# Layer 0's input projection as a one-level Strassen product, with the sums of the weights kept in DRAM

## The chip, the cores and the metric

The kernel runs on one core of one Trainium2 chip. The metric is the device time of one execution in microseconds (us); a kernel's time is the median of its runs. Names of engines follow the profile: PE is TensorE (PEld its weight loads), DVE is VectorE, ACT is ScalarE, POOL is GpSimd, SP is the queue from which all transfers are issued.

## The reference, cut to what matters

One step of a decoder trunk with two layers, all in float32, over 4096 prompt rows and 8 rows of samples, 1024 wide. The change is in layer 0:

```python
def even_layer(x, pool_prefix, conv_prefix, pos0, g_norm, w_in, pool_w, pool_scale, conv_w, w_out):
    h = rms_norm(x, g_norm)
    p = jnp.einsum('btd,de->bte', h, w_in)               # 1024 -> 3072
    u, z_a, b_gate, c_gate, v_in, z_b = jnp.split(p, EVEN_SPLITS, axis=-1)   # 512 each
    d = pool_mix(u, pool_prefix, pos0).reshape(B, T, N_POOL_GROUPS, POOL_GROUP)
    y_a = jnp.einsum('btgc,gce->btge', d, pool_w).reshape(B, T, W_POOL) * pool_scale * jax.nn.silu(z_a)
    v = c_gate * v_in
    y_b = b_gate * short_conv(v, conv_prefix, conv_w) * jax.nn.silu(z_b)
    y = jnp.einsum('bte,ed->btd', jnp.concatenate([y_a, y_b], axis=-1), w_out)
    ...
    return x + y, new_pool, new_conv
```

`pool_mix` is a trailing mean over 2, 4, 8 or 16 rows, by group of 128 channels; `short_conv` has three taps along the rows. Layer 1 is sliding-window attention with its own projections; its code is the same before and after.

## The kernel before

Every float32 operand of a product is split into two parts (`split`: ACT rounds it to the high part, DVE subtracts that to get the low part, L69 and L72), and a product is three matmuls: high by high, high by low, low by high.

Layer 0 goes through the 4096 rows in six chunks (`L1_CHUNKS`), of 512, 768, 768, 768, 640 and 640 rows; the 8 samples ride with the first. For each chunk, three stages follow one another:

- `prep`: 128 rows at a time are loaded, normed (ACT squares and sums, POOL makes the reciprocal root in `rstd`, DVE scales by it and by the gain row `gb`), transposed by PE eight blocks at a time, and split into `hh` and `hl`, channels on the partitions, rows along the free side.
- `mixers`: in each of four groups, six blocks of 128 output columns are projected (`block`: lines 259 to 261). A block loads a granule of weights (1024 by 128, 512 KB, buffers `wr`, three of them), splits it (`wh`, `wl`, four each), and multiplies it with the chunk in two pieces of at most 512 columns, 24 matmuls each. A piece is gathered in a PSUM bank `ps`, and ACT or DVE takes it from there into the pooling, the convolution and the gates. `psd` is the small block-diagonal product of the pooling branch. The result is split into `yh` and `yl`.
- `outproj`: the chunk's output projection (lines 385 to 389), 512 columns wide, with eight granules of `w_out` per chunk. While it runs, `prep` of the next chunk runs as well: its transposes stand between the output products on PE.

A scheduler sets the order of each engine's instructions when the kernel is built; each engine then works strictly in its order and waits at an instruction whose inputs are not there. Buffers are rings: a new tile waits until the old one in its place is done with.

Of the kernel before, what the change touches and what calls it, by code (L numbers as in the profile page):

```python
# [54 lines left out]
def hybrid_kernel(  # L55
# [85 lines left out]
    # ------------------------------------------------------------------ layer 0  # L141
    with ExitStack() as l1:
# [10 lines left out]
        gb = c1.tile([P, D], F32, tag="gb", name="gb")  # L153

        def load_w(src, shape, raw=None):
            if raw is None:
                raw = wp.tile([P, *shape], F32, tag="wr", name="wr", bufs=3)
                sp.dma_start(raw, src)
            wh = wp.tile([P, *shape], F32R, tag="wh", name="wh", bufs=4)
            wl = wp.tile([P, *shape], F32R, tag="wl", name="wl", bufs=4)  # L160
            split(wh, wl, raw)
            return wh, wl
# [44 lines left out]
        first_w = []  # L207

        def prep(ci):
            t0, n = L1_CHUNKS[ci]  # L210
            cols = n + (NS if ci == 0 else 0)
            hh = hp.tile([P, KT, cols], F32R, tag="hh", name="hh")
            hl = hp.tile([P, KT, cols], F32R, tag="hl", name="hl")
            for i in range(n // P):
                if not early:
                    xt = xp.tile([P, D], F32, tag="x", name="xt", bufs=2)
                    sp.dma_start(xt, xp_flat[t0 + i * P:t0 + (i + 1) * P, :])
                else:
                    xt = early.pop(0)
                if ci == 0 and i == 0:  # L220
                    first_w.append(load_w(w_in[:, :, 0:P], [KT, P], first_raw))
                ht = xp.tile([P, D], F32, tag="hn", name="ht", bufs=1)
                normed(xt, ht, P, gb, sm, hl[:, :, i * P:(i + 1) * P])
                to_channels(ht, pt, hh, hl, i * P)
# [1005 lines left out]
```

## Time and profile before

| what | value |
| --- | --- |
| three runs | 3395.51, 3397.54, 3399.41 us |
| median | 3397.54 us |
| span of the profiled execution, first to last instruction | 3388.8 us |
| the median less that span (start and end around it) | 8.7 us |
| PE busy | 95% of the span |
| DVE, ACT, POOL busy | 64%, 50%, 22% |
| end of layer 0's last output product on PE | 1541.0 us |

The profiled execution's own time is not listed apart from the three runs; it is taken as its span and the 8.7 us around it, which makes the median. Busy time is the time in which at least one instruction runs on the engine. Matmuls overlap one another, so a busy PE does not say how fast it goes; the time of a matmul is read as the length of a stretch divided by the matmuls in it.

### The profile page before, as it was taken

How to read it: one execution, taken by the hardware profiler on the slowest of the kernel's cores; microseconds unless marked ns; L12 is line 12 of the kernel's file. 1: busy time of each engine (PE TensorE's matmuls, PEld its weight loads, DVE VectorE, ACT ScalarE, POOL GpSimd, SP SyncE). 2: the span in 40 equal slices, each digit the busy share in tenths (PEclk: the TensorE clock that was granted, in tenths of full speed). 3: DMA queues.
4: the chain of work that ended last, by engine and by line, in shares of the span. 5: the costliest groups of instructions: out<-in, count | busy, mean ns of one | idle time of the engine just before them, and what ended most of it. 6: DMA issues, size and time to landing. Idle time of an engine off the chain costs nothing.

```text
span 3388.8 us, 48608 instructions
## 1 busy us (share of the span) xinstructions
PE 3224.2 (95%) x17226; PEld 2797.9 (83%) x17226; DVE 2152.4 (64%) x4348; ACT 1682.7 (50%) x3930; POOL 742.5 (22%) x1183
## 2 busy tenths in 40 slices
PE   7999999999999999998989999999999999999877
PEld 7989989988998999996767778777777887776665
DVE  4544443443443453443698897988979889797863
ACT  3332222231222232223586785867858678575761
POOL 1000000000000000001233342533425334343420
PEclk9999999999999999999999999999999999999988
DMA  5352243234224224234312424224232242321212
GB/s 159 100 160 65 63 131 100 63 100 125 62 76 155 75 88 137 73 101 131 104 53 75 136 68 135 87 82 135 68 126 90 81 139 71 108 83 58 74 66 97
DMA packets 303421, 330.19 MB, mean 97 GB/s; under 512 B 21545, under 2 KB 208561, under 8 KB 303138
## 3 DMA queue, kind: packets, MB, share of 16 engines
q1 hardware_dynamic: 303177, 327.09, 30.8%
q8 instruction: 136, 2.23, 0.3%
q14 instruction: 108, 0.88, 0.1%
HBM read 293.04 MB, written 36.29 MB: 97 GB/s over the span
## 4 chain that ended last, share of the span: by engine, by line
PE 44%; DVE 16%; ACT 7%; DMA 5%; issue 3%; POOL 1%; SPq 1%; DVEq 0%; ACTq 0%; POOLq 0%
PE pst L539 6%; PE pst L540 6%; PE pst L541 6%; PE ps L259 5%; PE ps L261 5%; PE ps L260 5%; ACT s L808 3%; DVE wl L507 3%; PE pso L389 2%; PE pso L385 2%; PE pso L387 2%; DVE qt L72 1%; PE o L842 1%; DVE s L792 1%; DVE st L802 1%
## 5 line engine op out<-in xcount | busy, mean ns | idle before, releaser
L259 PE MATMUL ps<-hh,wh 128*128 128x384 f32 (+3 forms) x2304 | 732.8, 318 | 4.0 <-ACT wh L69 3.7
L261 PE MATMUL ps<-hh,wl 128*128 128x384 f32 (+3 forms) x2304 | 731.7, 318 | 1.0 <-DVE wl L72 1.0
L260 PE MATMUL ps<-hl,wh 128*128 128x384 f32 (+3 forms) x2304 | 732.2, 318 | 0.1
L69 ACT ACTIVATE wh<-wr 128x1024 fp32r<-128x1024 f32 (+1 forms) x320 | 281.3, 887 | 727.5 <-PE ps L260 330.1
L72 DVE TENSOR_TENSOR wl<-wr,wh 128x1024 fp32r<-128x1024 f32 (+1 forms) x320 | 321.2, 1012 | 369.8 <-ACT wh L69 347.7
L259 PEld LDWEIGHTS ps<-hh,wh 128*128 128x128 f32 x2304 | 434.3, 189 | 5.2 <-ACT wh L69 4.3
L261 PEld LDWEIGHTS ps<-hh,wl 128*128 128x128 f32 x2304 | 433.8, 188 | 1.5 <-DVE wl L72 1.5
L260 PEld LDWEIGHTS ps<-hl,wh 128*128 128x128 f32 x2304 | 434.2, 188 | 0.6 <-DVE hl L72 0.4
L507 DVE SCALAR_TENSOR_TENSOR wl<-wr,gt,wh 128x256 fp32r<-128x256 f32 (+1 forms) x448 | 278.1, 638 | 67.8 <-ACT wh L506 61.6
L539 PE MATMUL pst<-wh,hh 128*128 128x512 f32 x768 | 312.0, 406 | 0.5 <-DVE xr L75 0.4
L506 ACT ACTIVATE wh<-wr,gt 128x256 fp32r<-128x256 f32 (+1 forms) x448 | 250.8, 597 | 116.0 <-DMA wr<-in_w_in_odd_dram 66.7
L541 PE MATMUL pst<-wl,hh 128*128 128x512 f32 x768 | 304.4, 396 | 0.0
L540 PE MATMUL pst<-wh,hl 128*128 128x512 f32 x768 | 303.9, 396 | 0.0
L808 ACT ACTIVATE s<-s,st,rq 128x128 f32<-128x128 f32 x512 | 246.9, 483 | 34.0 <-DVE st L804 32.3
L828 POOL TENSOR_SCALAR_AFFINE_SELECT qh<-ph 128x512 fp32r<-128x512 f32 x124 | 90.3, 728 | 688.4 <-ACT ph L69 669.9
L627 PE MATMUL psz<-hh,wh 128*128 128x512 f32 x512 | 211.6, 413 | 6.7 <-ACT wh L506 6.7
L539 PE MATMUL pst<-wh,yh 128*128 128x512 f32 x512 | 211.6, 413 | 3.9 <-DVE xr L75 3.8
L385 PE MATMUL pso<-wh,yh 128*128 128x512 f32 x512 | 202.7, 396 | 5.3 <-DVE xr L75 4.9
L628 PE MATMUL psz<-hl,wh 128*128 128x512 f32 x512 | 207.1, 405 | 0.0
L629 PE MATMUL psz<-hh,wl 128*128 128x512 f32 x512 | 206.5, 403 | 0.0
L541 PE MATMUL pst<-wl,yh 128*128 128x512 f32 x512 | 204.8, 400 | 0.0
L540 PE MATMUL pst<-wh,yl 128*128 128x512 f32 x512 | 204.7, 400 | 0.0
(265 smaller groups left out, 6577.7 us busy)
## 6 DMA issues: line engine op xcount, KB each, us to landing
wr<-in_w_in_odd_dram SPq DMA_DIRECT2D x320, 256.0 KB
wr<-in_w_in_even_dram SPq DMA_DIRECT2D x144, 512.0 KB
wr<-in_w_out_odd_dram SPq DMA_DIRECT2D x128, 256.0 KB
wr<-in_w_out_even_dram SPq DMA_DIRECT2D x48, 512.0 KB
xr<-in_x_prompt_dram SPq DMA_DIRECT2D x64, 256.0 KB
x<-xr SPq DMA_DIRECT2D x64, 256.0 KB
xt<-x SPq DMA_DIRECT2D x32, 512.0 KB
xr<-x SPq DMA_DIRECT2D x64, 256.0 KB
```

The lines of the kernel that those rows point to most:

```text
L69: return act.activation(out, in_, AF.Copy)
L72: return dve.tensor_tensor(out=out, in0=a, in1=b, op=ALU.subtract)
L259: pe.matmul(ps, lhsT=wh[:, kt, :], rhs=xh, start=kt == 0, stop=False)
L260: pe.matmul(ps, lhsT=wh[:, kt, :], rhs=xl, start=False, stop=False)
L261: pe.matmul(ps, lhsT=wl[:, kt, :], rhs=xh, start=False, stop=kt == KT - 1)
L385: pe.matmul(acc[i], lhsT=yh[:, kt, ts_], rhs=wh[:, e, :], start=kt == 0, stop=False)
L506: act.activation(wh[ix], raw[ix], AF.Copy, scale=gt[:, kt:kt + 1])
L507: dve.scalar_tensor_tensor(out=wl[ix], in0=raw[ix], scalar=gt[:, kt:kt + 1], in1=f(wh[ix]), op0=ALU.mult, op1=ALU.subtract)
L539: pe.matmul(acc[i], lhsT=xh(kt), rhs=wh, start=kt == 0, stop=False)
L540: pe.matmul(acc[i], lhsT=xl(kt), rhs=wh, start=False, stop=False)
L541: pe.matmul(acc[i], lhsT=xh(kt), rhs=wl, start=False, stop=kt == KT - 1)
L808: C["exp"] = act.activation(s[:, h, :], s[:, h, :], AF.Exp, bias=nm[:, h:h + 1], scale=r4[:, h:h + 1], accum_out=den[:, h:h + 1])
```

## The change

The input projection of layer 0 is done as one level of Strassen's scheme (in Winograd's form). Two blocks of 128 output columns, the two halves of the 1024 channels, and the two halves of a chunk's rows make a 2 by 2 by 2 product of quarters; 8 quarter products become 7, with sums of quarters as operands. A chunk has 12 such pairs of blocks (`pair`), and each quarter product is 4 channel tiles by 3 matmuls, over half of the chunk's rows at once.

- The rows' side: `prep` makes seven operands of a pair of row tiles (`B11`, `B21`, `B22` and the sums `T1` to `T4`), in `operand_cols`, and splits each.
- The weights' side: `operands` makes four granules of a pair, `A11` and `A12`, `S2` and `S1`, `S3` and `S4`, `A22` (the last has half the size). In the first chunk it loads the two blocks, multiplies them by the norm's gain on POOL (`scaled`; the gain row `gb` on the rows' side is gone), makes the sums on DVE and POOL, splits them, and writes all seven quarters to DRAM (`wsc`). Later chunks load the seven quarters from there.
- The outputs: within a pair, bank `px` goes on being added to after it has been copied (by ACT: `p1`, `u2`; bank `pz` gives `p5`), and three of the four results are sums that DVE makes (`out11`, `out22`, `out12`); the fourth is `px` at the end.
- Chunks are 768, 768, 768, 768, 512 and 512 rows (`L0_CHUNKS`), so products are 384 columns wide in the first four (388 with the samples) and 256 in the last two. `wh` and `wl` have three buffers each, not four.

```diff
-L1_CHUNKS = [(0, 512), (512, 768), (1280, 768), (2048, 768), (2816, 640), (3456, 640)]
+L0_CHUNKS = [(0, 768), (768, 768), (1536, 768), (2304, 768), (3072, 512), (3584, 512)]
...
+        def scaled(raw):
+            v = raw.rearrange("p a k e -> p (a k) e")
+            pool.tensor_tensor(out=v, in0=v, in1=g0.unsqueeze(2).to_broadcast([P, KT, P]),
+                               op=ALU.mult)
...
+        def operands(ci, pair, blocks):
+
+            if ci > 0:
+                out = []
+                for i in range(4):
+                    raw = raw_tile()
+                    n = 1 if i == 3 else 2
+                    sp.dma_start(raw[:, :n], wsc[pair][:, 2 * i:2 * i + n])
+                    out.append(parts(raw[:, :n]))
+                return out
+            ra = first_w.pop(0) if first_w else load_block(blocks[0])
+            scaled(ra)
+            ga = parts(ra)
+            rb = first_w.pop(0) if first_w else load_block(blocks[1])
+            scaled(rb)
+            s12 = xp.tile([P, 2, 4, P], F32, tag="x", name="s12", bufs=2)
+            s34 = xp.tile([P, 2, 4, P], F32, tag="x", name="s34", bufs=2)
+            add(s12[:, 1], rb[:, 0], rb[:, 1])
+            sub(s12[:, 0], s12[:, 1], ra[:, 0])
+            pool.tensor_tensor(out=s34[:, 0], in0=ra[:, 0], in1=rb[:, 0], op=ALU.subtract)
+            sub(s34[:, 1], ra[:, 1], s12[:, 0])
+            sp.dma_start(wsc[pair][:, 0:2], ra)
...
+                b12 = temp("b12", 1)
+                acopy(b12, quad(0, 1))
+                q = quad(0, 0)
+                split(bh[:, 0, :, cs], bl[:, 0, :, cs], q)
+                t1 = temp("t4", 2)
+                sub(t1, b12, q)
+                q = quad(1, 1)
+                split(bh[:, 2, :, cs], bl[:, 2, :, cs], q)
+                t2 = temp("t4", 2)
+                sub(t2, q, t1)
+                part(0, t1)
+                t3 = temp("t4", 2)
+                sub(t3, q, b12)
+                part(1, t2)
+                part(2, t3)
+                q = quad(1, 0)
+                split(bh[:, 1, :, cs], bl[:, 1, :, cs], q)
+                t4 = temp("t4", 2)
+                sub(t4, q, t2)
+                part(3, t4)
...
-                        pe.matmul(ps, lhsT=wh[:, kt, :], rhs=xh, start=kt == 0, stop=False)
-                        pe.matmul(ps, lhsT=wh[:, kt, :], rhs=xl, start=False, stop=False)
-                        pe.matmul(ps, lhsT=wl[:, kt, :], rhs=xh, start=False, stop=kt == KT - 1)
...
+                    for kt in range(4):
+                        for i, (u_, v_) in enumerate(((wh, xh), (wh, xl), (wl, xh))):
+                            pe.matmul(ps, lhsT=u_[:, at, kt, :], rhs=v_[:, o, kt, :],
+                                      start=start and kt == 0 and i == 0, stop=kt == 3 and i == 2,
+                                      skip_group_check=True)
...
+                x = bank("px")
+                mm(x, "A11", "B11", start=True)
+                p1 = kept(x, "p1")
+                y = bank("py")
+                mm(y, "A12", "B21", start=True)
+                out11(y, p1)
+                if mid is not None:
+                    mid()
+                mm(x, "S2", "T2")
+                u2 = kept(x, "u2")
+                z = bank("pz")
+                mm(z, "S1", "T1", start=True)
+                p5 = kept(z, "p5")
+                mm(x, "S3", "T3")
+                out22(x, p5)
+                mm(z, "S4", "B22")
+                out12(z, u2)
+                mm(x, "A22", "T4")
+                return x
```

Three places in the order of the engines, first POOL at the program's start. `rnt` and `rnr` are the two steps of a row tile's reciprocal root, `u` and `vv` carry rows over from the last piece, and before the change the order there is this:

```order
L105 TENSOR_SCALAR rnt<-ss 128x1
L274 COPY u<-ucar 128x15
L326 COPY vv<-vcar 128x2
L109 TENSOR_TENSOR rnr<-rnt,mh 128x1
L105 TENSOR_SCALAR rnt<-ss 128x1
L109 TENSOR_TENSOR rnr<-rnt,mh 128x1
```

After the change, with L197 the multiplication of a weight block by the gain:

```order
L105 TENSOR_SCALAR rnt<-ss 128x1
L197 TENSOR_TENSOR wr<-wr,g_139 128x1024
L109 TENSOR_TENSOR rnr<-rnt,mh 128x1
L105 TENSOR_SCALAR rnt<-ss 128x1
L427 COPY u<-ucar 128x15
L109 TENSOR_TENSOR rnr<-rnt,mh 128x1
L197 TENSOR_TENSOR wr<-wr,g_139 128x1024
```

The multiplication of the first weight block has come between the two steps of the first row tile's reciprocal root; 24 of them stand in the first chunk's part of POOL's order, two to a pair of blocks.

The second place is PE at the program's start, before the change (`tr` and `trs` are the transposes of row tiles and of the samples):

```order
L260 MATMUL ps<-hl,wh 128x256
L261 MATMUL ps<-hh,wl 128x256
L130 MATMUL tr<-ident,ht 128x128 x8
L138 MATMUL trs<-ident,hts 128x8 x8
L259 MATMUL ps<-hh,wh 128x264
L260 MATMUL ps<-hl,wh 128x264
```

After the change, the first rows of all:

```order
L334 MATMUL tr<-ident,xe 128x128 x16
L334 MATMUL tr<-ident,xt 128x128 x32
L138 MATMUL trs<-ident,xs_344 128x8 x8
L373 MATMUL px<-bh,wh 128x388
L373 MATMUL px<-bl,wh 128x388
L373 MATMUL px<-bh,wl 128x388
```

Before, the first piece's products (256 wide) stand between the transposes, after 16 of them; now all 48 transposes and those of the samples stand ahead of the first product, since a product takes half of the chunk at once.

The third place is DVE in a late chunk, in the convolution's blocks of a group, before the change (640 rows, pieces 320 wide; the words in brackets name the engines that the instruction waits for):

```order
L72 TENSOR_TENSOR wl<-wr,wh 128x1024 [waits DMAHW4_49,Activation_49]
L333 SCALAR_TENSOR_TENSOR t<-vv,cw,t 128x320 [waits DVE_49] x2
L78 TENSOR_TENSOR t<-t,zb 128x320 [waits Activation_49]
L72 TENSOR_TENSOR wl<-wr,wh 128x1024 [waits DMAHW7_49,PE_49,Activation_49]
L78 TENSOR_TENSOR t<-t,zb 128x320 [waits DVE_49,Activation_49]
L78 TENSOR_TENSOR y<-ps,t 128x320 [waits DVE_49,PE_49]
```

After the change (512 rows, 256 wide; `yb<-px,p` is `out22` of a pair, `zb<-pz,u` its `out12`):

```order
L72 TENSOR_TENSOR wl<-wr,wh 128x512 [waits DMAHW4_49,PE_49,Activation_49]
L75 TENSOR_TENSOR zb<-py,p_10371 128x256
L78 TENSOR_TENSOR t<-t,zb 128x256 [waits Activation_49]
L72 TENSOR_TENSOR wl<-wr,wh 128x1024 [waits DMAHW5_49,PE_49,Activation_49]
L75 TENSOR_TENSOR yb_10431<-px,p_10417 128x256 [waits PE_49,Activation_49]
L75 TENSOR_TENSOR zb<-pz,u_10402 128x256 [waits PE_49]
L72 TENSOR_TENSOR wl<-wr,wh 128x1024 [waits DMAHW6_49,Activation_49]
```

New are the sums from the banks, and a weight split stands right ahead of `out22`, for which PE's last product of the pair (into `px` again) has to wait; before, a bank was written once and the next piece had another.

## Rows read from the trace of the kernel before

**Rows 1.** The page: the span and each engine's busy time over it.

```profile
span 3388.8 us, 48608 instructions
...
PE 3224.2 (95%) x17226; PEld 2797.9 (83%) x17226; DVE 2152.4 (64%) x4348; ACT 1682.7 (50%) x3930; POOL 742.5 (22%) x1183
```

**Rows 2.** Stretches of layer 0: us, each engine's busy time (instructions), granted clock, DMA.

```profile
core 0: us, PE busy (x) PEld busy (x) DVE busy (x) ACT busy (x) POOL busy (x), PEclk, DMA share, GB/s
120.00:170.00 50.00, 50.00 (x420) 50.00 (x419) 29.09 (x64) 14.96 (x29) 3.04 (x12) 1.00 0.29 86
237.91:442.00 204.09, 204.09 (x1178) 204.09 (x1177) 88.76 (x134) 51.10 (x81) 12.39 (x32) 1.00 0.24 72
442.00:518.04 76.04, 72.87 (x336) 58.11 (x336) 30.70 (x36) 21.96 (x34) 5.19 (x12) 1.00 0.46 146
1313.10:1485.71 172.61, 172.61 (x1179) 172.54 (x1178) 81.77 (x133) 47.10 (x80) 10.27 (x30) 1.00 0.29 87
1486.33:1541.03 54.70, 54.70 (x245) 45.25 (x243) 13.85 (x20) 10.17 (x20) 2.83 (x9) 1.00 0.34 115
```

**Rows 3.** The timeline's start: start us, us, engine, line, operation, tiles, [idle before <-releaser].

```profile
...
0.80 0.38 SPq L416 DMA_DIRECT2D xe<-in_x_prompt_dram  x1
...
4.38 1.06 ACT L120 ACTIVATE hl<-xe 128x1024 fp32r<-128x1024 f32 x1 [2.30 <-DMA xe<-in_x_prompt_dram]
...
6.76 1.28 DVE L122 SCALAR_TENSOR_TENSOR ht<-xe,rnr,gb 128x1024 f32<-128x1024 f32 x1 [6.76 <-POOL rnr L109]
...
8.10 1.97 PE L130 MATMUL tr<-ident,ht 128*128 128x128 f32 x8 [8.10 <-DVE ht L122]
...
9.77 1.06 ACT L69 ACTIVATE wh<-wr 128x1024 fp32r<-128x1024 f32 x1 [0.73 <-DMA wr<-in_w_in_even_dram]
...
15.79 0.58 PE L259 MATMUL ps<-hh,wh 128*128 128x256 f32 x1
```

**Rows 4.** VectorE groups by shape, layer 0: count | busy us, mean ns | idle before, releasers.

```profile
L72 DVE TENSOR_TENSOR wl<-wr,wh 128x1024 fp32r<-128x1024 f32 x192 | 234.2, 1222 | 307.3 <-ACT wh L69 301.4 <-DMA x<-xr 3.4 <-ACT hh L69 2.2
...
L72 DVE TENSOR_TENSOR hl<-tr,hh 128x512 fp32r<-128x512 f32 x64 | 41.3, 682 | 2.9 <-ACT hh L69 2.8
...
L78 DVE TENSOR_TENSOR vv<-ps,c 128x384 f32<-128x384 f32 x24 | 13.4, 558 | 38.5 <-PE ps L261 38.5
...
L78 DVE TENSOR_TENSOR vv<-ps,c 128x256 f32<-128x256 f32 x8 | 3.4, 425 | 5.9 <-PE ps L261 5.9
...
L579 DVE TENSOR_SCALAR xt<-xt,rnr 128x1024 f32<-128x1024 f32 x3 | 2.3, 754 | 3.0 <-POOL rnr L109 3.0
```

**Rows 5.** ScalarE groups by shape, layer 0, same columns.

```profile
L69 ACT ACTIVATE wh<-wr 128x1024 fp32r<-128x1024 f32 x192 | 202.8, 1059 | 627.5 <-PE ps L260 330.1 <-PE pso L387 195.8 <-issue 63.9
...
L69 ACT ACTIVATE c<-ps 128x384 f32<-128x384 f32 x24 | 11.6, 482 | 34.2 <-PE ps L261 34.2
...
L69 ACT ACTIVATE c<-ps 128x256 f32<-128x256 f32 x4 | 1.5, 381 | 5.5 <-PE ps L261 5.5
```

**Rows 6.** GpSimd instructions of three kinds: duration ns min/median/max.

```profile
L656 POOL TENSOR_TENSOR tab<-raw,gq x132: 309/326/1104, 1556.7 to 3191.7; 128x64 f32<-128x64 f32 x128, 8x64 f32<-8x64 f32 x4
...
L326 POOL COPY vv<-vcar x48: 186/187/194, 6.0 to 1468.9; 128x2 f32<-128x2 f32 x48
...
L828 POOL TENSOR_SCALAR_AFFINE_SELECT qh<-ph x124: 630/637/1627, 1709.5 to 3334.6; 128x512 fp32r<-128x512 f32 x124
```

**Rows 7.** A piece of the timeline in layer 1, VectorE and GpSimd.

```profile
2005.06 1.20 DVE L507 SCALAR_TENSOR_TENSOR wl<-wr,gt,wh 128x512 fp32r<-128x512 f32 x1
2005.08 0.63 POOL L828 TENSOR_SCALAR_AFFINE_SELECT ql<-pl 128x512 fp32r<-128x512 f32 x1
...
2005.78 0.97 POOL L830 TENSOR_SCALAR_AFFINE_SELECT pl<-pl 128x512 fp32r<-128x512 f32 x1
```

**Rows 8.** Two VectorE lines of layer 1: duration ns min/median/max.

```profile
L507 DVE SCALAR_TENSOR_TENSOR wl<-wr,gt,wh x448: 446/544/1196, 1544.8 to 3229.8; 128x256 fp32r<-128x256 f32 x86, 128x512 fp32r<-128x512 f32 x64
...
L792 DVE COPY_PREDICATED s<-pmask,sc x248: 407/440/461, 1695.4 to 3302.4; 128x256 f32<-128x256 uint8 x124
```

More of the change, by code (lines that the diff above doesn't have):

```diff
@@ L151, in hybrid_kernel @@
         pt = l1.enter_context(tc.tile_pool(name="pt1", bufs=2, space=PSUM))
[L153 to L162, printed above, removed]
         w_in = w_in_even[0].rearrange("(k p) e -> p k e", p=P)
         w_out = w_out_even[0].rearrange("(k p) e -> p k e", p=P)
+        wsc = [dram.tile([P, 7, 4, P], F32, tag=f"wsc{i}", name=f"wsc{i}") for i in range(12)]
+        AT = {"A11": (0, 0), "A12": (0, 1), "S2": (1, 0), "S1": (1, 1), "S3": (2, 0), "S4": (2, 1),
+              "A22": (3, 0)}
+        g0 = c1.tile([P, KT], F32, tag="g0", name="g0")
         pwl = c1.tile([P, 4, P], F32R, tag="pwl", name="pwl")
@@ L205, in setup_sample, with x_norm0 @@
             sp.dma_start(nconv_s[0][:, 0:1], state_conv[0][:, 1:2])
-        first_w = []
-        def prep(ci):
[L210 to L224, printed above, removed]
+        def x_norm0(xt, n, junk):
+            ss = sm.tile([P, 1], F32, tag="ss", name="ss")
+            act.activation(junk[:n], xt[:n].rearrange("p (k c) -> p k c", c=P), AF.Square,
+                           accum_out=ss[:n])
+            r = rstd(ss[:n], n, 1, 1.0 / D, EPS, sm, "rn")
+            dve.tensor_scalar(out=xt[:n], in0=xt[:n], scalar1=r[:n, 0:1], scalar2=None, op0=ALU.mult)
@@ L322, in mixers, with into, silu_, out_z2 @@
-                ts_ = []
-                for pi, c0, w, L, ps in block(16 + g):
-                    vv = tp.tile([P, 2 + WX], F32, tag="vv", name="vv")
-                    c = cs_[pi]
+                    split(dh, dl, d)
+                    return dh, dl
+                def into(t):
+                    return lambda a, b: add(t, a, b)
+                def silu_(t, src):
+                    act.activation(t, src, AF.Silu)
+                def out_z2(a, b):
+                    add(zs[1], a, b)
+                    silu_(zs[1], zs[1])
@@ new lines, in mixers, with linear @@
+                c21 = pair(3 * g, (g, 4 + g), into_u(0), into_u(1), out_z2)
+                silu_(zs[0], c21)
+                ds_ = [pooled(0), pooled(1)]
+                def linear():
+                    for pi in range(2):
+                        ps = bank("psd")
+                        dh, dl = ds_[pi]
+                        pe.matmul(ps, lhsT=pwh[:, g, :], rhs=dh, start=True, stop=False)
+                        pe.matmul(ps, lhsT=pwh[:, g, :], rhs=dl, start=False, stop=False)
+                        pe.matmul(ps, lhsT=pwl[:, g, :], rhs=dh, start=False, stop=True)
+                        put_y(g, pi, lambda o: dve.scalar_tensor_tensor(
+                            out=o, in0=ps, scalar=psc[:, g:g + 1], in1=zs[pi], op0=ALU.mult,
+                            op1=ALU.mult))
@@ new lines, in mixers, with out_v2 @@
+                cs_ = [tp.tile([P, WX], F32, tag="c", name="c") for _ in range(2)]
+                vs = [tp.tile([P, 15 + WX], F32, tag="uv", name="vv") for _ in range(2)]
+                def out_v2(a, b):
+                    add(vs[1][:, 2:2 + w], a, b)
+                c21 = pair(3 * g + 1, (12 + g, 16 + g), into(cs_[0]), into(cs_[1]), out_v2, linear)
+                ts_ = []
+                for pi in range(2):
+                    vv, c = vs[pi], cs_[pi]
+                    src = c21 if pi == 0 else vv[:, 2:2 + w]
+                    if hs:
+                        mul(stc[:, g, pi * hs:pi * hs + hs, 2], src[:, L:w], c[:, L:w])
+                    mul(vv[:, 2:2 + L], src[:, :L], c[:, :L])
```

247 lines of the change are left out of this document (151 added, 96 removed).

## The prediction

> **What bounds the kernel now.** I read first the page: PE is busy for 95% of the span [rows 1]. A busy PE may still be slow, so next I read stretches of layer 0, stage by stage [rows 2]. In a chunk's projection (237.91 to 442.00 us and 1313.10 to 1485.71 us stand for three stretches of 204.1 us and two of 172.6 us) PE is busy without a gap, while DVE works 88.8 of 204.1 us and the transfers fill a quarter of their engines: PE alone bounds this stage, and fewer matmuls shorten it. In an output projection (442.00 to 518.04 us) PE is idle for 3.2 us. Then the start of the timeline [rows 3]: transposes begin at 8.10 us, the first product at 15.79 us. Last I read the durations by shape of what the change adds on DVE, ACT and POOL [rows 4 to 6], and what happens when DVE and POOL work at once [rows 7, 8].
>
> **PE's products.** A chunk of 768 rows has 1152 projection matmuls and 24 of the pooling branch; two of the row's 1178 only overlap its ends. 204.09 us by 1176 is 173.5 ns for 384 columns, 172.61 by 1176 is 146.8 ns for 320, so a column costs 0.417 ns. 50.00 us by 420 is 119.0 ns for the first chunk's mix of 256 and 264 columns; I take 118 ns for 256 and 175.2 ns for 388 [rows 2]. After the change a chunk has 12 pairs by 7 products by 12 matmuls, 1008, and the 24: 180.8 us for the first chunk, 3 by 179.1 for the next, 2 by 121.8 for the last two, 961.6 us in all. Before, it was 1176 by 119.0 = 139.9, 612.3 and 345.2, together 1097.4 us; the first chunk's stage ended at 177.5 us (where the following stages, back from 1541.0, leave it), so 37.6 us of it was start and stalls. This term is **-135.8 us**. That is 12.4%, close to one product in eight; the granted clock reads 1.00 in all of these stretches and changes nothing in it.
>
> **The start, 37.6 us before.** POOL now multiplies a weight block between the two steps of the first tile's reciprocal root. That block was there at 9.77 us before, three transfers of 512 KB behind the first row tile's 4.38; that is 1.8 us each, and with the broadcast gain row gone I put it at 8.0. A multiplication of 1024 columns is not in the trace. From below it costs two of the one-input passes over 512, 1.26 us; from above I scale the two-input one: 309 ns for 64 columns against 187 ns for a copy of 2 is 2.0 ns a column, 2.2 us [rows 6]. I take 2.2, the same kind of instruction. The root's two steps fill the time from the squares' end, 5.44, to 6.76, so the second is some 0.6; with 0.75 for the scaling this puts the first transposes near 11.7 us, not 8.1. All six tiles and the samples must be done before the first product. A pair of tiles costs DVE eleven passes of 0.68 and two of 0.75, 9.0 us [rows 4]; if nothing overlapped, the 7.3 us from a tile's issue to its transposes [rows 3] would come on top, 16.3. The two row buffers let most of the loading hide, so I take 10.5: 11.7 + 31.5 + 4 for the samples is 47 us (41 to 65). Term: **+9.4**.
>
> **The first chunk.** DVE's work per chunk is the 88.8 us of before, plus 12 by (3 by 1.22 + 0.69) less 24 by 1.22 for the splits of weights, +22.9, plus 36 sums from banks at 0.56, +20.1: 131.8 us of 179.1, so DVE has room in the middle chunks. The first chunk adds 36 sums of weights at 0.68 and some 70 small instructions for the samples, each below the 0.43 of a 256-wide one, which I put at 10 us together: 166 of 180.8. And POOL has 24 multiplications and 12 differences (1.2), 67 us, and 6 us of copies. In layer 1, a DVE instruction of line 507 that starts at 2005.06 takes 1.20 us, against a median of 0.54: POOL's, which ends at 2005.71, is in its way, and POOL's next, at 2005.78, takes 0.97 instead of 0.63 [rows 6, 7]. Line 507 reads two SBUF tiles and ranges from 446 to 1196 ns; line 792 takes its data from a PSUM bank and never exceeds 461 [rows 8]. So the two engines exclude each other on such instructions. Of the 166 us, the sums and the other readers of a bank are 29, the rest 137. If POOL's 73 us hide behind those 29 as well as they can, the stage takes 137 + 73 = 210 us; with no hiding 239; with POOL at its lower price (24 by 1.26, 12 by 0.63, 6 of copies) 181, PE's own time. I take 220, nearer to 210 because POOL works most of a pair ahead of PE. Term: **+39.2** over 180.8.
>
> [...]
>
> **Middle chunks.** A pair hands banks back and forth: ACT's copy of `pz` and DVE's `out22` must be done before PE comes back. From the end of S1 by T1: ACT first splits a granule (1.06), DVE makes its low part (1.22), then `out22` (0.56), about 3.05 us with the waits between; PE is back in `px` after two products of 2.08, 4.16. ACT's copy is done at 1.75, before 2.08 [rows 4, 5]. It is hidden with 1.1 us to spare. I take **+6** for three chunks; a late DVE would cost more (below).
>
> **Late chunks.** The same at 256 columns: a product is 1.42 us, ACT's copy is done at 1.65, so PE loses 0.25 in each of 24 pairs, 6 us. DVE's work other than weight splits shrinks with the width (0.558 at 384, 0.425 at 256, 0.49 between): 81.8 - 29.3 = 52.5 at 320 becomes 45.4; with 52.3 of splits and 36 by 0.425 it is 113 us of 121.8, 93%. So near its limit it will be late at times; I take **+14** in all (6 to 40).
>
> **Between chunks.** `prep` costs DVE 9.0 us for a pair of tiles instead of two by (1.28 + 2 by 0.68), 5.3; for three pairs 11 us more, 42 of an output stage's 76. It stays under, but the transposes stand early in PE's order: 3 us more idle at each of five ends, **+14** (0, if the order hides it, to 48, if nothing of DVE's is hidden). ACT gains as much as DVE in splits and starts from 51 of 204, so it stays clear. Layer 1's code is the same.
>
> **Sum.** -135.8 + 9.4 + 39.2 + 6 + 14 + 14 = -53.2. The profiled span of 3388.8 becomes 3335.6; with the 8.7 us that the median has over it, **3344 us**.
>
> **Rival: POOL is not in the way.** If the multiplications are cheap or hide, the first chunk takes some 186 us: 34 less, 3310 us. For it: POOL was nearly idle there (12 us of 204) and the scheduler puts the scalings a pair ahead. Against: [rows 7].
>
> **Rival: the handing back of banks costs every pair, and the kernel is slower.** At `px` PE waits for `out22`, which stands behind a weight split that itself waits for PE and ACT. If DVE is x late, PE loses about x - 1.1 in each of 48 wide pairs and x in 24 narrow ones. 20 us of this is in the sum, so it takes 73 us to lose the gain, x = 1.75: a split and a sum behind (1.22 + 0.56). Two splits behind, 2.4 us, gives 3441 us. For it: in the late chunks DVE has 9 us to spare in 122. Against: 74% in the middle ones, where most pairs are.
>
> **Rival: the transfers.** Each later chunk loads 22 MB of weights, not 12.6: 181 GB/s in a late chunk. Busy shares of 0.24 at 72 and 0.46 at 146 GB/s give 0.6 for it [rows 2]. If 146 were the most, the late chunks would take 151 us each, 3402 us in all.
>
> **Rival: the bad ends.** No hiding in the first chunk (+19) and a start at 65 (+18): 3381 us.
>
> **Chances.** The forecast 0.48 (own range 3320 to 3365), POOL not in the way 0.20, the bad ends 0.17, the banks 0.10, the transfers 0.05. The range 3290 to 3392 takes in the forecast, POOL and the bad ends; left out are about 0.05 below and 0.13 above. Within 0.2%, about what a measurement of this kernel can tell from no change, is 3390.7 to 3404.3. Faster 0.85, same 0.05, slower 0.10.
>
> **What would show it.** First product near 47 us. First chunk's projection near 220 us with POOL's multiplications over 2 us and DVE's splits stretched beyond 1.22. Middle ones at 179 to 183 with few gaps, late ones near 129, with PE waiting for `out22` or `pz`'s copy. Layer 0's last product near 1488 us, not 1541. It is wrong if middle chunks show a gap in every pair, or if the first is at PE's pace.

## The result, and the profile after

The changed kernel takes 3352.32 us (median of 4 runs, 3348.26 to 3354.68), the kernel before, run beside it, 3398.47 us (3395.51 to 3402.22). The ratio is 0.9859, with a 95% interval of 0.9845 to 0.9873: faster by 1.4%, some 46 us. The forecast was 3344 us.

The page of the changed kernel, its span and the engines' busy time, which answers to [rows 1]:

```profile
span 3352.4 us, 48712 instructions
...
PE 3131.0 (93%) x16362; PEld 2687.0 (80%) x16362; DVE 2471.7 (74%) x4914; ACT 1892.4 (56%) x4277; POOL 860.1 (26%) x1219
```

PE's share fell from 95% to 93% and DVE's rose from 64% to 74%. Stretches of layer 0, which answer to [rows 2]: the start, the first chunk's projection and the output stage behind it, a middle projection, a late one, and the last output stage.

```profile
core 0: us, PE busy (x) PEld busy (x) DVE busy (x) ACT busy (x) POOL busy (x), PEclk, DMA share, GB/s
0.00:53.54 53.54, 13.38 (x57) 9.92 (x57) 30.29 (x44) 24.31 (x43) 14.92 (x44) 1.00 0.53 167
53.54:283.62 230.08, 203.89 (x1048) 196.63 (x1049) 183.90 (x314) 85.11 (x154) 79.76 (x65) 0.93 0.46 155
283.62:368.63 85.01, 81.33 (x371) 61.70 (x369) 43.33 (x66) 30.45 (x51) 6.01 (x12) 1.00 0.43 137
368.63:550.48 181.85, 181.77 (x1034) 180.97 (x1032) 125.18 (x193) 80.55 (x123) 19.62 (x32) 1.00 0.44 134
1146.91:1274.61 127.70, 126.23 (x1033) 123.30 (x1032) 104.03 (x191) 70.36 (x122) 17.92 (x32) 1.00 0.61 189
1453.33:1498.20 44.87, 44.87 (x197) 36.39 (x195) 15.72 (x25) 11.42 (x22) 2.84 (x9) 1.00 0.45 149
```

The middle projections fell from 204.1 to 181.9 us and PE has no gap in them; the late ones, now 512 rows wide, take 127.7 us. The first is the odd one. It has the same products as a middle one, four columns wider, and takes 230.1 us: PE is idle for 26.2 us of it, and the granted clock is 0.93. DVE and POOL are both far from full there (183.9 and 79.8 of 230.1 us), so a share of busy time does not explain it. Layer 0 ends at 1498.2 us, before at 1541.0; layer 1 takes 1854.2 us, before 1847.8.

The start, to be held against [rows 3], on POOL:

```profile
start us, us, engine line op out<-in xcount [idle before <-releaser]
...
5.69 0.19 POOL L105 TENSOR_SCALAR rnt<-ss 128x1 f32<-128x1 f32 x1 [3.40 <-ACT tl L272]
8.29 1.90 POOL L197 TENSOR_TENSOR wr<-wr,g 128x1024 f32<-128x1024 f32 x1 [2.41 <-DMA wr<-in_w_in_even_dram]
10.14 0.57 POOL L109 TENSOR_TENSOR rnr<-rnt,mh 128x1 f32<-128x1 f32 x1
...
12.30 1.90 POOL L197 TENSOR_TENSOR wr<-wr,g 128x1024 f32<-128x1024 f32 x1
```

On DVE, the scalings of the first two row tiles:

```profile
10.74 0.75 DVE L275 TENSOR_SCALAR xe<-xe,rnr 128x1024 f32<-128x1024 f32 x1 [10.74 <-POOL rnr L109]
12.36 2.38 DVE L275 TENSOR_SCALAR xe<-xe,rnr 128x1024 f32<-128x1024 f32 x1 [0.87 <-POOL rnr L109]
```

On PE, the first transposes of the three pairs of tiles, those of the samples, and the first product:

```profile
11.55 1.12 PE L334 MATMUL tr<-ident,xe 128*128 128x128 f32 x4 [11.55 <-DVE xe L275]
...
26.71 1.08 PE L334 MATMUL tr<-ident,xt 128*128 128x128 f32 x4 [7.61 <-DVE xt L275]
...
36.62 1.09 PE L334 MATMUL tr<-ident,xt 128*128 128x128 f32 x4 [4.17 <-DVE xt L275]
...
52.14 0.99 PE L138 MATMUL trs<-ident,xs 8*128 8x8 f32 x8 [8.08 <-DVE xs L275]
53.54 0.69 PE L373 MATMUL px<-bh,wh 128*128 128x388 f32 x1 [0.41 <-ACT bh L69]
```

The first scaling of a weight block (L197) stands between the two steps of the first root, as the order showed, and took 1.90 us. The second shows the exclusion at once: from 12.30 to 14.20 POOL multiplies, and DVE's scaling of a row tile, 0.75 us just before, takes 2.38.

In the first chunk's projection, POOL's largest group (count | busy us, mean ns | idle before, releasers):

```profile
L197 POOL TENSOR_TENSOR wr<-wr,g 128x1024 f32<-128x1024 f32 x21 | 48.3, 2304 | 80.0 <-DMA wr<-in_w_in_even_dram 54.4 <-DVE t L78 5.7 <-DVE t L499 4.2
```

DVE's three largest groups by shape there:

```profile
L72 DVE TENSOR_TENSOR wl<-s,wh 128x1024 fp32r<-128x1024 f32 x24 | 32.6, 1359 | 2.9 <-ACT wh L69 2.8
L72 DVE TENSOR_TENSOR wl<-wr,wh 128x1024 fp32r<-128x1024 f32 x11 | 16.0, 1451 | 9.2 <-ACT wh L69 9.2
L75 DVE TENSOR_TENSOR s<-wr 128x512 f32<-128x512 f32 x11 | 13.7, 1244 | 0.0
```

In [rows 4] a weight split took 1222 ns; here the mean is 1359 and 1451. A sum of two weight quarters that should cost as much as a split of 512 columns, 682, takes 1244.

Part of the 26 us of idle PE is one stop. The waits of SP, the transfers' queue, from 30 to 100 us (us in total, times, longest):

```profile
engine line waited for: us in total, times, longest us
SPq L254 <- DVE pwl L72: 17.9, 1, 17.9
SPq L242 <- DVE t L72: 14.8, 1, 14.8
```

The stretches around it, columns as in the stretches above:

```profile
69.50:77.50 8.00, 7.97 (x46) 7.64 (x44) 1.92 (x5) 2.06 (x5) 0.60 (x1) 1.00 0.00 0
77.50:93.50 16.00, 6.34 (x19) 4.07 (x20) 10.71 (x15) 5.08 (x16) 5.64 (x3) 0.56 0.57 174
93.50:101.50 8.00, 8.00 (x39) 8.00 (x38) 4.90 (x9) 2.54 (x5) 4.12 (x4) 0.80 0.73 214
```

L242 loads the pooling weights `pw`, L254 the pooling state `sp_raw`. The change put both into the single buffer `b12` that the row work uses too. They shared one buffer before as well, but then `pw` was loaded at 8.51 us and `sp_raw` waited 1.7 us for its split. Now `pw` itself waits 14.8 us for the row work and is loaded at 57.71, so its split falls into the projection, and `sp_raw` waits 17.9 us for it. Behind `sp_raw` in SP's order stand the second pair's weight loads. So nothing is transferred from 69.5 to 77.5 us (DMA 0.00), PE runs dry, and for 16 us it is busy for 6.3 us at a granted clock of 0.56, close to 0.50, the lower of its two levels (1.2 of 2.4 GHz). Back at work it is at 0.80 for 8 us more.

### The profile page after: what moved, and what is told of

It is laid out like the page before. It is cut to its first block, busy times and chain, and to the rows that moved or that the text cites. A ratio compares the mean times of both kernels' runs of the same rounds, so it can differ in the third digit from the quotient of the medians.

```text
span 3352.4 us, 48712 instructions
## 1 busy us (share of the span) xinstructions
PE 3131.0 (93%) x16362; PEld 2687.0 (80%) x16362; DVE 2471.7 (74%) x4914; ACT 1892.4 (56%) x4277; POOL 860.1 (26%) x1219
## 4 chain that ended last, share of the span: by engine, by line
PE 23%; DVE 15%; ACT 7%; DMA 5%; issue 3%; POOL 1%; SPq 1%; DVEq 0%; ACTq 0%; POOLq 0%
PE pst L720 6%; PE pst L721 6%; PE pst L722 6%; ACT s L989 3%; DVE wl L688 2%; DMA wr<-in_w_in_odd_dram 2%; DVE qt L72 1%; PE o L1023 1%; DVE s L973 1%; DMA xr<-x 1%; PE sc L965 1%; DMA out_dram<-xr 1%; DVE st L983 1%; DVE ot L75 1%; ACT wh L687 1%
## 5 line engine op out<-in xcount | busy, mean ns | idle before, releaser
L69 ACT ACTIVATE wh<-wr 128x512 fp32r<-128x512 f32 (+1 forms) x392 | 327.6, 840 | 448.5 <-PE pz L373 125.0
L72 DVE TENSOR_TENSOR wl<-wr,wh 128x512 fp32r<-128x512 f32 (+1 forms) x392 | 373.2, 960 | 214.9 <-ACT wh L69 194.0
L688 DVE SCALAR_TENSOR_TENSOR wl<-wr,gt,wh 128x256 fp32r<-128x256 f32 (+1 forms) x448 | 277.3, 637 | 69.5 <-ACT wh L687 67.5
L373 PE MATMUL px<-th,wh 128*128 128x384 f32 (+2 forms) x864 | 280.1, 324 | 9.8 <-DVE za L75 6.4
L373 PE MATMUL px<-th,wl 128*128 128x384 f32 (+2 forms) x864 | 278.7, 323 | 0.0
L373 PE MATMUL px<-tl,wh 128*128 128x384 f32 (+2 forms) x864 | 278.7, 323 | 0.0
L570 PE MATMUL pso<-who,yh 128*128 128x512 f32 x512 | 204.7, 400 | 5.6 <-DVE xr L75 5.5
L572 PE MATMUL pso<-who,yl 128*128 128x512 f32 x512 | 204.3, 399 | 0.0
L574 PE MATMUL pso<-wlo,yh 128*128 128x512 f32 x512 | 202.7, 397 | 0.0
L428 POOL COPY ucar<-u 128x15 f32<-128x15 f32 x48 | 26.4, 550 | 611.0 <-DVE u L75 599.2
```

The source lines that it names most:

```text
L69: return act.activation(out, in_, AF.Copy)
L72: return dve.tensor_tensor(out=out, in0=a, in1=b, op=ALU.subtract)
L373: pe.matmul(ps, lhsT=u_[:, at, kt, :], rhs=v_[:, o, kt, :], start=start and kt == 0 and i == 0, stop=kt == 3 and i == 2, skip_group_check= ...
L688: dve.scalar_tensor_tensor(out=wl[ix], in0=raw[ix], scalar=gt[:, kt:kt + 1], in1=f(wh[ix]), op0=ALU.mult, op1=ALU.subtract)
```

## The experiments

Two theories stood at first. The forecast's: POOL's multiplications and DVE's instructions with two SBUF inputs **exclude** each other. Its rival A: the multiplication is only a longer **chain** from a weight's load to its product. "Projection" means the first chunk's, from its first product to its first output product. Stage times are those of a kernel's one profiled execution; e2, e3, e4, e5, e8 and e10 ran once only. For a measure of their noise: the middle projections, the same in all kernels but e8, lie between 181.3 and 182.5 us. To make room, all kernels but e3, e4 and e8 keep the output stages' `xr` tiles in the buffers of the `c` tiles.

**The gain back on the rows (e1).**

```diff
-            scaled(ra)
...
-            scaled(rb)
...
-            dve.tensor_scalar(out=xt[:n], in0=xt[:n], scalar1=r[:n, 0:1], scalar2=None, op0=ALU.mult)
+            dve.scalar_tensor_tensor(out=xt[:n], in0=xt[:n], scalar=r[:n, 0:1], in1=gb[:n],
+                                     op0=ALU.mult, op1=ALU.mult)
```

> The norm gain goes back to the row tiles (a broadcast gain row, one scalar_tensor_tensor for a tile); POOL keeps the twelve s34 differences and its small copies. Theory (POOL's 24 scalings and DVE's passes with two SBUF operands shut each other out): the first chunk's projection falls from 230.1 to 182 to 195 us, DVE's weight splits there go back from 1.36 to 1.45 us to below 1.30, the first product moves from 53.5 to 48 to 51 us, the whole kernel takes 3300 to 3315 us. Rival A (POOL's time is only a link in the chain from a weight's load to its product): the same, this run does not tell it apart. Rival B (DVE's own work, the stores and the weight ring set the stage): 215 us or more, 3335 us or more.

Measured: 3318.58 us, ratio 0.9771 (0.9755 to 0.9788); projection 194.7 us, DVE's splits 1216 and 1220 ns, first product at 54.3 us. Taking POOL's scaling away gives the splits their old price and the stage 35 us, part of it, as e9 will show, for another reason; at 194.7 rival B is out. The start did not move to 48 to 51; the two-input scaling of a row tile (1.28 us in [rows 3], for 0.75) may cost about what POOL's wait had cost, which no run shows.

**The multiplication beside the chain (e2).**

```diff
-            pool.tensor_tensor(out=v, in0=v, in1=gains, op=mult)
+            pool.tensor_tensor(out=aside, in0=aside, in1=gains, op=mult)
```

> POOL's 24 multiplications of 128x1024 by the gains are made on a tile of their own that nothing else reads, so they are in no chain; the weights stay without the layer-0 gain. Theory (exclusion): the work still shuts DVE out, the first chunk's projection stays at 215 to 232 us with DVE's splits stretched as in the changed kernel. Rival A (a link in the chain): 182 to 195 us, as without the scaling.

Measured: projection 197.0 us, but this run, outside both expectations, tells nothing apart. With no input to wait for, all 24 multiplications (2023 ns each, 48.6 us) ran before the first product, which came at 81.0 us. A later run mends it.

**Fills in the chain, reading nothing (e3).**

```diff
-            pool.tensor_tensor(out=v, in0=v, in1=gains, op=mult)
+            pool.memset(v, 0.02)
+            pool.memset(v, 0.01)
```

> Each multiplication is replaced by two fills of the same 128x1024 weight tile with constants, also on POOL and at the same place in the chain; they read nothing (the weights of layer 0 are then constants). Theory (exclusion through what POOL reads): DVE's weight splits go back below 1.30 us and the first chunk takes 182 to 200 us, though POOL still stands between a load and its splits. Rival A (a link in the chain): with fills of about 1 us each it stays at 215 us or more. If DVE's splits stay stretched, fills shut DVE out as well.

Measured: two fills take 955 and 954 ns, together as long as a multiplication alone (1.90 us). Projection 201.5 us, DVE's splits 1217 and 1306. Not the 215 of rival A, but above the theory's 200.

**The gain on ACT (e4).**

```diff
-            pool.tensor_tensor(out=v, in0=v, in1=gains, op=mult)
+            for kt in range(KT):
+                act.activation(v[:, kt], v[:, kt], AF.Copy, scale=g0[:, kt:kt + 1])
```

> The weights are scaled in place by ACT, eight activations of 128x128 with the gain as a scale per partition for each block, some 0.25 us each, 48 us more on ACT in the first chunk (85 before); POOL keeps the s34 differences. Theory (exclusion): 185 to 200 us for the first chunk, ACT near 135 us busy, the kernel at 3305 to 3325 us. Rival A (a link in the chain): the chain is as long as before (about 2 us), so 215 us or more.

Measured: 3321.83 us (one run), projection 205.6 us, ACT busy 132.9 us, splits 1219 and 1218, first product at 50.6 us. DVE is at its old prices in these splits, but the stage is longer than in e1 and outside the range. In e3 and e4 PE waited 4.4 us for `sp_raw`, about as in the changed kernel (4.6), in e1 0.9 us: the stop at the setup's load was a third suspect.

**The same multiplication, result unused (e5).** It reads each arriving block, as before.

```diff
-            pool.tensor_tensor(out=v, in0=v, in1=gains, op=mult)
+            pool.tensor_tensor(out=aside, in0=v, in1=gains, op=mult)
```

> POOL still multiplies each arriving weight block by the gains, 24 times 128x1024, reading the block, but writes the product to a tile that nothing uses; the splits and sums take the unscaled block, so the multiplication is in no chain (layer 0 without its gain). In e2 the same work had no input to wait for and ran ahead in the start; here it can't. Theory (exclusion): the first chunk's projection takes 215 to 232 us, with POOL near 80 us busy and DVE's splits above 1.30 us. Rival A (a link in the chain): 190 to 205 us.

Measured: projection 215.8 us, POOL 77.7 us busy, DVE's two weight splits 1216 and 1760 ns. No product waits for these multiplications, and they still cost the stage some 20 us over e1 and e2, as exclusion has it. The run is not wholly clean: a multiplication still holds the weight buffer that it reads, POOL's differences stand behind it, and of the two splits only one is above the 1.30 us expected of both.

**Nothing large on POOL at all (e6).**

```diff
-            pool.tensor_tensor(out=s34[:, 0], in0=ra[:, 0], in1=rb[:, 0], op=subtract)
+            sub(s34[:, 0], ra[:, 0], rb[:, 0])          # on DVE; the gain on the rows as in e1
```

> The gain on the row tiles as in e1, and the twelve s34 differences go from POOL (1.79 us each, 21.5 us) to DVE (0.68 each, 8.2 us). Theory (exclusion): what is left of the first chunk's excess was POOL's 21.5 us shutting DVE out; the stage falls from 194.7 to 186 to 192 us and the kernel to 3308 to 3316 us (e1: 3318.6). Rival B (DVE's own load sets the rest): DVE has 8 us more to do and the stage is at 195 to 203 us.

Measured: 3309.54 us, ratio 0.9753 (0.9734 to 0.9771); projection 186.8 us. DVE took over 8 us of work and the stage became shorter, against rival B once more:

```profile
53.87:240.68 186.81, 186.81 (x1048) 185.28 (x1049) 157.89 (x326) 85.65 (x154) 13.97 (x32) 0.99 0.58 193
```

DVE's same three groups in it:

```profile
L72 DVE TENSOR_TENSOR wl<-s,wh 128x1024 fp32r<-128x1024 f32 x24 | 29.2, 1218 | 1.2 <-ACT wh L69 1.1
L72 DVE TENSOR_TENSOR wl<-wr,wh 128x1024 fp32r<-128x1024 f32 x11 | 13.5, 1223 | 4.9 <-ACT wh L69 4.9
...
L75 DVE TENSOR_TENSOR s<-wr 128x512 f32<-128x512 f32 x11 | 7.5, 685 | 0.0
```

PE has no gap left, and each of DVE's groups is back at its price alone (1359 to 1218, 1451 to 1223, the 512-wide sum 1244 to 685).

**The sample rows early (e7).**

```diff
                 operand_cols(i * P, P, quad)
+                if ci == 0 and i == 0:
+                    samples()               # was behind the third pair of tiles
```

> e6 with the eight sample rows prepared behind the first pair of row tiles and not behind the third, in a weight buffer. Theory on the start (a chain of in-order waits on ACT and DVE from tile to tile, not their amount of work): with the samples' chain of some 5 us off the end, the first product moves from about 54 to 48 to 51 us and the kernel gains 3 to 5 us on e6. Rival C (DVE's and ACT's amount of work sets the start): within 1 us of e6.

Measured: 3315.30 us, ratio 0.9771 (0.9756 to 0.9785), no gain on e6, against the 3 to 5 us expected. The first product came at 47.4 us, 6.4 earlier, so the start was a chain, and rival C is out; but the projection grew to 202.6 us, with a stop of 4.5 us at `sp_raw`.

**An eighth product (e8).**

```diff
                 mm(y, "A12", "B21", start=True)
+                mm(y, "A12", "B21", start=True)
```

> The changed kernel with one product of each pair (A12 by B21) done twice, so eight products for seven, all else as it was. If PE's products set the middle and late stages, each middle chunk rises by 144 matmuls at 176 ns, 25.3 us, to 207 us and each late one by 144 at 118 ns, 17 us, to 145 us. Theory for the first chunk (POOL and DVE set it): it rises by less than PE's 25.6 us, by 3 to 15 us. Whole kernel: 3352 + 76 + 34 + 3 to 15, 3465 to 3478 us. Rival: if the first chunk is set by the chain ahead of each pair, it rises by the whole 25 us.

Measured: 3474.94 us (one run). Middle projections 207.5, 207.0 and 207.4 us, late ones 142.7 and 143.3 us: one product in eight is worth 25.4 us in a middle chunk and 15.3 in a late one. The first rose by 18.1 us, to 248.2, more than the theory's 3 to 15 and less than PE's 25:

```profile
53.90:302.09 248.19, 222.23 (x1193) 215.68 (x1193) 175.86 (x314) 84.72 (x154) 73.91 (x65) 0.96 0.44 144
```

PE is idle for 248.2 - 222.2 = 26.0 us, as with seven products (26.2). More work for PE did not fill the waits, so the stage is not set by the sum of DVE's and POOL's work, as by full engines. That leaves single hand-overs that come late; e9 and e10 will show which. With eight products the kernel is slower than before (3474.94 against 3393.61 us beside it).

**The setup's tiles in buffers of their own (e9).** Here the gain is on POOL, as in the change.

```diff
-            pw = tp.tile([P, 4, P], F32, tag="b12", name="pw", bufs=1)
+            pw = tp.tile([P, 4, P], F32, tag="c", name="pw")       # and sp_raw, sc_raw
```

> The changed kernel, gain on POOL as it was, but the pooling weights and the two state tiles of the setup no longer share the one buffer of the row work's b12 tile; they take the two buffers of the conv branch's c tiles, free until then. In the changed kernel the state load waited 17.9 us on SyncE for that buffer with the next weight blocks queued behind it, PE ran dry at 77 us and its granted clock fell to half. Theory in two parts (POOL's exclusion some 28 us of the first chunk, this one stop 10 to 18 us): the first chunk's projection falls from 230.1 to 210 to 220 us, no stop near 78 us, the kernel at 3333 to 3343 us. Rival D (the stop is made up again, since POOL and DVE set the stage): 226 us or more, 3348 us or more.

Measured: 3343.12 us, ratio 0.9843 (0.9828 to 0.9858); projection 215.9 us, no wait for `sp_raw`, and rival D is out. The start came 3.7 us later (57.2). By the profiles layer 0 ends at 1483.5 us, 14.7 earlier than in the changed kernel, 10.5 of it by the end of this projection; the two ratios' intervals overlap, so for the whole time the gain is not settled.

**Fills, with those buffers (e10).**

```diff
-            pool.tensor_tensor(out=v, in0=v, in1=gains, op=mult)
+            pool.memset(v, 0.02)
+            pool.memset(v, 0.01)
...
-            pw = tp.tile([P, 4, P], F32, tag="b12", name="pw", bufs=1)
+            pw = tp.tile([P, 4, P], F32, tag="c", name="pw")
```

> e3 (two fills on POOL in place of each multiplication, so the chain keeps its length and POOL reads nothing) with the buffers of e9. Theory in two parts: what e3 had over e6 (201.5 against 186.8 us) was the stop at the setup's load, not the longer chain; the first chunk now takes 185 to 192 us. Rival A (the chain): 196 to 202 us, as in e3.

Measured: projection 190.9 us. Its text differs from e9's only in what POOL does in the chain. First the stretch in e10:

```profile
54.70:245.61 190.91, 187.49 (x1047) 184.37 (x1045) 161.25 (x311) 84.51 (x153) 70.39 (x86) 1.00 0.55 186
```

POOL's two lines of fills in it:

```profile
L197 POOL MEMSET wr<- 128x1024 f32 x21 | 20.2, 961 | 80.4 <-DMA wr<-in_w_in_even_dram 33.4 <-DVE s L72 8.6 <-DVE yb L78 7.7
L198 POOL MEMSET wr<- 128x1024 f32 x21 | 20.0, 954 | 1.0
```

DVE's two groups of weight splits in it:

```profile
L72 DVE TENSOR_TENSOR wl<-s,wh 128x1024 fp32r<-128x1024 f32 x24 | 29.2, 1217 | 1.2 <-ACT wh L69 1.1
L72 DVE TENSOR_TENSOR wl<-wr,wh 128x1024 fp32r<-128x1024 f32 x11 | 13.4, 1221 | 4.5 <-ACT wh L69 4.5
```

Now the same stretch in e9:

```profile
57.24:273.12 215.88, 195.27 (x1046) 189.16 (x1045) 184.87 (x311) 84.27 (x153) 76.06 (x65) 0.98 0.49 164
```

and DVE's weight splits in e9:

```profile
L72 DVE TENSOR_TENSOR wl<-s,wh 128x1024 fp32r<-128x1024 f32 x24 | 33.8, 1408 | 2.8 <-ACT wh L69 2.8
L72 DVE TENSOR_TENSOR wl<-wr,wh 128x1024 fp32r<-128x1024 f32 x11 | 20.0, 1818 | 3.9 <-ACT wh L69 3.9
```

PE's waits in e9:

```profile
engine line waited for: us in total, times, longest us
PE px L373 <- DVE za L75: 9.0, 4, 2.7
PE pz L373 <- ACT p L69: 4.3, 3, 2.2
PE px L373 <- DVE yb L75: 3.3, 3, 1.4
```

and in e10:

```profile
PE psd L476 <- DVE dl L72: 1.2, 2, 0.8
PE pz L373 <- ACT p L69: 0.9, 2, 0.5
PE px L373 <- DVE za L75: 0.6, 1, 0.6
```

One such hand-over on DVE in e9:

```profile
70.54 2.95 DVE L72 TENSOR_TENSOR wl<-wr,wh 128x1024 fp32r<-128x1024 f32 x1
...
73.88 0.55 DVE L75 TENSOR_TENSOR za<-px,p 128x388 f32<-128x388 f32 x1
```

POOL is busy for 70.4 us in the one and 76.1 in the other, at the same place in the chain. What differs is reading: DVE 161.3 against 184.9 us, its splits 1217 and 1221 against 1408 and 1818 ns, the stage 25.0 us. The waits show how that reaches PE: `za<-px,p` and `yb<-px,p` are `out22`. At 70.54 us in e9 a split takes 2.95 us, `out22` stands behind it, and PE's next product into `px` starts at 74.48, after a wait of 1.6 us. In all PE waits 12.3 us for `out22` in e9, 0.6 in e10. Rival A is out: with a chain of the old length the stage is 4.1 us over e6, and part of that is the twelve differences, still on POOL.

The scheduler could have placed things differently in the two. In the traces, PE's products and transposes come in the same order in e9 and e10, and ACT's order differs at two places by a step or two, DVE's within a few groups by a few instructions, SP's by one place at five loads. Between e3 and the change, which differ in the same way and by 28.6 us, the orders of PE and ACT are equal, DVE's differs at two places, and SP's at some loads and stores. So the order is no likely cause of either difference.

**The best parts together, twice (e11 and e12).**

```diff
-            pw = tp.tile([P, 4, P], F32, tag="b12", name="pw", bufs=1)
+            pw = tp.tile([P, 4, P], F32, tag="c", name="pw")       # in e7, and sp_raw, sc_raw
```

> e7 (gain on the rows, no POOL differences, sample rows early) with the buffers of e9. Theory in two parts: e7 lost its earlier start again only at the setup's load; the first product stays near 47.5 us, the first chunk takes 185 to 190 us and not 202.6, the kernel 3299 to 3306 us, below e6. Rival D: the stage is at 198 us or more whatever the load does.

```diff
-            pool.tensor_tensor(out=v, in0=v, in1=gains, op=mult)
+            for kt in range(KT):
+                act.activation(v[:, kt], v[:, kt], AF.Copy, scale=g0[:, kt:kt + 1])
...
-            pool.tensor_tensor(out=s34[:, 0], in0=ra[:, 0], in1=rb[:, 0], op=subtract)
+            sub(s34[:, 0], ra[:, 0], rb[:, 0])
...
+                if ci == 0 and i == 0:
+                    samples()
...
-            pw = tp.tile([P, 4, P], F32, tag="b12", name="pw", bufs=1)
+            pw = tp.tile([P, 4, P], F32, tag="c", name="pw")
```

> The weights are scaled by ACT as in e4, the twelve differences are on DVE, the sample rows early, the buffers of e9: POOL has only its small copies. The row tiles need no broadcast gain (0.75 us in place of 1.28 for a tile). Theory in two parts: first product at 42 to 46 us, first chunk 185 to 192 us, the kernel 3295 to 3303 us. Rival A (the chain through ACT costs as in e4): the first chunk 198 us or more.

Measured: 3311.25 us, ratio 0.9754 (0.9739 to 0.9768), and 3317.44 us, ratio 0.9774 (0.9758 to 0.9791). The first products came at 46.9 and 44.2 us, but the projections took 199.3 and 204.4 us: both expectations missed, and what e7 lost was not the setup's load alone. At 80 us PE waits 4.9 us for a high part of the second pair. A piece of DVE's timeline in e11, at the first pair's end:

```profile
74.16 0.56 DVE L75 TENSOR_TENSOR c<-py,p 128x388 f32<-128x388 f32 x1 [3.35 <-PE py L370]
...
77.06 0.68 DVE L75 TENSOR_TENSOR s<-wr 128x512 f32<-128x512 f32 x1
77.67 0.68 DVE L72 TENSOR_TENSOR s<-wr 128x512 f32<-128x512 f32 x1
```

The same part of DVE's work in e6:

```profile
63.02 0.69 DVE L75 TENSOR_TENSOR s<-wr 128x512 f32<-128x512 f32 x1
...
64.16 0.68 DVE L72 TENSOR_TENSOR s<-s,wr 128x512 f32<-128x512 f32 x1
...
64.84 0.68 DVE L72 TENSOR_TENSOR s<-wr 128x512 f32<-128x512 f32 x1
...
76.32 0.55 DVE L75 TENSOR_TENSOR c<-py,p 128x388 f32<-128x388 f32 x1
```

The second pair's sums (`s<-wr`, `s<-s,wr`) start at 63.02 us in e6, among the first pair's sums from banks; in e11 they stand in DVE's order behind the sum `c<-py`, which waited 3.35 us for PE, and start at 77.06. The scheduler had placed them differently. That this order is the whole loss is read from the timeline, not tried. e6, with e11 level to it within the intervals, is the fastest kernel, 1.1% under the change (0.9753 by 0.9859).

## Why the prediction was right, and which terms were off

The direction, the size and the likeliest case held. Term by term, by the profiled executions (3335.6 us forecast as the span, 3352.4 measured):

| term | forecast, us | measured, us |
| --- | --- | --- |
| start, to the first product | 47 | 53.5 |
| first chunk's projection | 220 | 230.1 |
| three middle projections | 543.2 | 545.5 |
| two late projections | 257.6 | 255.4 |
| stages between | 420 | 413.7 |
| layer 1 | 1847.8 | 1854.2 |
| median over the span | 8.7 | -0.1 |

**PE's products**: right. Middle and late projections together are 0.1 us off, and e8 prices an eighth product at 25.4 and 15.3 us (forecast, 144 by 173.5 and by 118 ns: 25.0 and 17.0). Seven for eight is where the gain comes from: with eight, e8 has none.

**The start**: mis-sized by 6.5 us. The first transposes came at 11.55 us, as worked out (11.7). The three pairs and the samples then took 42.0 us, not 35.5. By e7 the samples at the end cost 6.4 us, not 4, which leaves 11.9 us for a pair and not 10.5. In e4, where ACT scales the weights, the first product comes 2.9 us earlier (50.6 against 53.5), so by about that much POOL's scaling holds up the start.

**The first chunk**: the mechanism was right, the working behind the size was not. I added DVE's 137 us and POOL's 73 us to a bound of 210 and took 220, as if the stage were limited by two full engines. Four runs split what happened:

| projection, us | no stop at `sp_raw` | stop at `sp_raw` |
| --- | --- | --- |
| POOL fills (of its large work only the differences read) | 190.9 (e10) | 201.5 (e3) |
| POOL multiplies (excludes DVE) | 215.9 (e9) | 230.1 (the change) |

Exclusion costs 25.0 to 28.6 us, the stop 10.6 to 14.2; without the stop the first product came 2.4 us (e10) and 3.7 us (e9) later, so 8.2 and 10.5 us of that are won by the end of the stage. From e6 up to the change: 186.8, plus 4.1 for the chain and the differences on POOL, plus 25.0, plus 14.2, is 230.1. This is one path through four kernels and not four clean prices: e1, with the differences on POOL and no chain, took 194.7, more than e10 with both. Of the 43.3 us between e6's stage and the change's, 26.2 are idle PE and 17.1 are longer busy time for the same 1048 matmuls (203.9 against 186.8 us), in part at a lower granted clock (0.93 against 0.99). Exclusion acts by making DVE late for single hand-overs, `out22` above all (e9 against e10). The whole stage without the stop, 215.9, lies in the forecast's 210 to 220 more by its bounds than by its model. One reading was loose: I held the 1.20 us of an instruction of line 507 against a median of 0.54 that mixes two widths; its 512-wide instructions alone have a median of 0.74, which it still exceeds. The stop itself was not in the forecast: the diff showed `pw` and `sp_raw` moving to the tag `b12`, and I did not follow what waits behind them in SP's order.

The Trainium skill's page "SBUF — State Buffer", section "Who interferes with whom", says that DVE with two SBUF inputs contends with a GpSimd instruction that reads SBUF and not with one that only writes it. Fills and multiplications of equal length agree (splits of 1217 and 1221 ns against 1408 and 1818).

**Middle and late chunks**: the sizes of the terms held (+8.3 measured for +6, +11.8 for +14), their reason only in part. In a middle projection PE is busy for 181.77 of 181.85 us, so the excess over 179.1 is a slower rate, 176.2 ns a matmul (181.85 by 1032) for 173.5, and not a wait for a bank; why is open. In a late one 1.5 us are idle and the rate is 123.7 ns for 118; the profile lists 0.7 us of waits there, so the handing back of banks that I had put at 6 us is not shown to be the reason. In e8 the 144 matmuls added to a late chunk cost 106 ns each (15.3 us by 144), under the rate of the rest, so some pause between products was there to be filled; which, stays open.

**Between chunks**: 413.7 us against 406 before; I had +14, it was +7.7. **Layer 1** began with waits of its first products for `wh` (9.8 us); its code is unchanged. **The median over the span**: I carried 8.7 us over, but the profiled execution of the changed kernel took 3354.14 us for a span of 3352.4, so what lies around a span is 1.7 us. If that holds before as well, the profiled execution there took some 3390.5 us, less than any of the runs listed beside it, and 7 of the 8.7 us were that difference. This error and that of the span, +16.8, partly cancel: that the median is only 8.3 us off where the span is 16.8 off is luck.

**The rivals.** POOL not in the way: its condition was false, but its price for the stage was right. I put that stage at 186 us and that kernel at 3310; e6, in which POOL is out of the way, has 186.8 and 3309.54. The second match is partly luck: e6 starts 6.9 us later than the 47 in that sum, and of the 8.7 us around the span it has 1.8. The banks: no middle or late chunk shows a wait for `out22`, so the kernel isn't bound by it there; but a late DVE does hold up `px` in the first chunk (5.5 us in the change, 12.3 in e9), which I had not tied to exclusion. By its own terms that rival's 2.4 us of lateness makes 3444 us, not 3441. The transfers: 189 GB/s flow in a late one, more than the 146 at which that rival had set its limit. The bad ends did not come together.

## What to carry to other kernels

Before work is given to an idle POOL, look at what it reads: a multiplication there cost DVE time (e9), as fills of the same length did not (e10), and in a stage where DVE hands over to PE that time comes back as stops. When a change makes tiles share a buffer, follow the load that waits for it and all that stands behind it in the transfers' queue. Time won at a start is kept only if the order of the engines behind it, fixed when the kernel is built, can use it.

## What the runs showed of the hardware that was not expected

DVE's scaling of a row tile (tensor_scalar, one SBUF input, 128x1024) is excluded as well: 0.75 us alone, 2.38 us with POOL's multiplication in its way. I had counted only instructions with two SBUF inputs. The Trainium skill's page "SBUF — State Buffer", section "Who interferes with whom", lists `tensor_scalar` among the operations that can run in a mode with both port pairs and then contend. The trace agrees that it contends (2.38 against 0.75 us); which mode it ran in, no run shows.

One stop cost PE more than its idle time: over the 16 us in which PE was idle for most of the time, the granted clock read 0.56, and 0.80 over the next 8 us, in which PE was busy throughout and did 39 matmuls. In e6 it read 1.00 over 77.9 to 93.9 us, with 47 matmuls in each 8 us.
